# Gate and up products of the experts: stationary weights, 96 streamed slots, one-piece weight split

## The chip, the cores and the metric

One core of a Trainium2 chip runs the whole program. The metric is device time in microseconds of one execution; the median of three runs is quoted. The engines are called PE (matrix products, PEld for its weight loads), DVE (vector), ACT (scalar), POOL and SP (which issues the loads).

## The reference

Two layers over 256 latent and 256 context tokens of width 1024. Each layer has three attention branches merged by gates, then a channel mixer: a dense SwiGLU in layer 0, and in layer 1, for the latents alone, eight experts of which each token uses two:

```python
gate, up = jnp.split(h @ w_gu, 2, axis=-1)
return (jax.nn.silu(gate) * up) @ w_dn
```

Per expert w_gu is 1024 x 5632 and w_dn 2816 x 1024, in fp32. The router takes the top two of eight logits per token and weights the two outputs by a softmax over them. There are 512 assignments of a token to an expert. The result is the latents' stream after a last RMS norm.

## The kernel before, in words

Every matrix is held as two fp16 parts, high and low, and a product is three fp16 products: high by high, high by low, low by high. Weights come from memory as fp32 tiles of 128 x 2048 (1 MiB). `load_raw` (L300) issues the load on SP into the next of a ring of buffers, 12 in the expert stage. `split_w` (L308) makes the parts into one of three pairs of weight buffers (`WB`, L283): ACT writes the high part (L266), DVE the low part (L263), in two pieces of 1024 columns each. ACT, DVE and PE work on different tiles at once. The framework's planner sets each engine's order from the program; only in a few places (`issue_after`) is it written by hand.

The experts come last (L1106 to L1324). `route` (L1114) sorts tokens into slots. Then, one expert after the other:

- `gather` (L1176) builds a 0/1 matrix P of tokens by 128 slots, and with it the expert's tokens `xg`, two parts of [d, slots] (products at L1201, copies on ACT at L1203), the transposed matrix PT and the slots' weights `wsl`. The next expert's gather is called during this one's down products.
- `expert` (L1207) has 11 blocks of two weight tiles. A tile holds, for four chunks of the contraction, 256 gate and 256 up columns. The tokens are stationary (128 x 128) and 512 weight columns stream past them: 12 products a tile (L1227 to L1229), with the result [slots, 256 gate | 256 up] in one bank of PSUM. ACT takes SiLU of the gate half into `ht` (L1231), DVE multiplies by the up half (L1232, by the helper at L257). `turn` (L1213) puts the block's product on [hidden, slots] by two fp32 transposes on PE (L1216), and ACT and DVE split that into `hdh` and `hdl`. A block is turned only after the next one's products (`last`).
- Then 11 tiles of the down projection: `hdh`, `hdl` stationary, 512 columns streaming, 132 products (L1254 to L1256), and the scaled outputs `yh`, `yl` (L1258).
- `combine` (L1262) brings the outputs of up to three experts back to their tokens; its eight jobs are put between a later expert's blocks. The last expert's own follow each half of its result.

A second pass (L1327 to L1357) runs in a device loop over the experts, if some expert has more than 128 tokens.

```python
for k in range(4):
    kk = 4 * half + k
    c = slice(512 * k, 512 * k + 512)
    T.matmul(ps, xg[0][:, kk], w[0][:, c], start=(kk == 0), stop=False)
    T.matmul(ps, xg[0][:, kk], w[1][:, c], start=False, stop=False)
    T.matmul(ps, xg[1][:, kk], w[0][:, c], start=False, stop=(kk == KD - 1))
```

Of the kernel before, what the change touches and what calls it, by code (L numbers as in the profile page):

```python
# [15 lines left out]
D = 1024  # L16
# [5 lines left out]
NE = 8  # L22
VW = 416
# [9 lines left out]
# ---------------------------------------------------------------- layout of the inputs (host, no arithmetic)  # L33
# [116 lines left out]
def const_mats():  # L150
    """ident | rotation | one, heads | strictly lower | expert triangle | slots"""
# [58 lines left out]
def moe_tiles(w_gu, w_dn, w_router):  # L210
    """Per expert: 22 tiles of gate and up columns side by side, 11 tiles of the down projection, one half of its
    outputs after the other."""
    g = w_gu.reshape(NE, 2, 4, 128, 2, 11, 256)
    g = g.transpose(0, 5, 1, 3, 2, 4, 6).reshape(NE, 22, 128, 2048)
# [29 lines left out]
# ---------------------------------------------------------------- the kernel  # L244


def trunk(tc, A, out):
# [41 lines left out]
    def take(kind, slots):  # L289
        """The next of several groups of buffers, in proportion to their sizes."""  # L290
        order = [g for g in slots for _ in range(g[2])]
        g = order[turn[kind] % len(order)]
        turn[kind] += 1
        return g
# [13 lines left out]
    def split_w(raw, w, parts=None):  # L308
# [4 lines left out]
        for a in range(0, w, 1024):  # L313
            b = min(w, a + 1024)
# [13 lines left out]
    # ---- constants and small inputs  # L328
# [25 lines left out]
    # silu of the conditioning: as columns, and along every lane for the row sums  # L354
# [18 lines left out]
    def ada_tile(pool, cb, t):  # L373
        """Two column chunks of layer 1's modulation, for the latents' and (where used) the context's vector."""
# [10 lines left out]
    def ada_group(i, g):  # L385
        """The eight chunks of group g (sh1 sc1 g1 sh2 sc2 g2) are in: bias, then the form that the use needs."""
# [30 lines left out]
    def ada0_cols(row, ch):  # L417
        """The column groups' sum, put on the lanes, and the bias: chunks ch .. ch+3."""
# [7 lines left out]
    def first_mod(half):  # L426
        """Layer 0's first shift and scale, half of the chunks."""
# [128 lines left out]
    def residual(ps, d, c, gate, o=0):  # L556
        """xT chunk d, tokens c: plus the gated product."""
# [5 lines left out]
    def start(pool, nrm):  # L563
        """Layer 0's first norm and products, as its shift and scale come in."""
# [20 lines left out]
    def mixer(pool, i, ada_q, nrm, nxt, first=None):  # L585
        """One layer's three token mixers: adds the gated merge of their outputs to xT, and feeds the next norm."""
# [34 lines left out]
        # ---- first products, following the norm  # L621
# [39 lines left out]
        def bcast(rstd, tiles, s, two):  # L661
            """1/rms values of one norm, along the lanes of its chunk: [128, tokens] in PSUM."""
# [12 lines left out]
        def turned(dst, r, c):  # L675
            """The rotary turn of the latents."""
# [42 lines left out]
        # ---- values, and the rotary key of the latent-attention branch, token by token  # L719
# [32 lines left out]
        def gate0(d):  # L752
            """A chunk of the first branch's gate, kept where the merge goes."""
# [6 lines left out]
        class Latent:  # L760
            """The latent queries: projected, normed."""
# [22 lines left out]
        class Grouped:  # L784
            """Two chunks of the grouped-query branch: projected, normed by head, turned."""
# [24 lines left out]
        # ---- latent-attention branch: normed low ranks, then up  # L810
# [45 lines left out]
        # ---- attention: pairs of heads, context queries over the context, latent queries over everything  # L856
# [83 lines left out]
        # ---- a branch's output, gated (tanh of half the argument), added to the merge  # L940
# [165 lines left out]
    # ---- experts: 128 slots each; a second block of slots for the experts that are given more tokens  # L1106
# [69 lines left out]
    def gather(pool, pos_e, w_e, slots):  # L1176
        """One block of 128 slots of one expert: the scale of its outputs, its tokens in fp16 parts [d, slots], the slot
        matrix [slots, tokens]."""
        P = pool.tile([128, 2, 128], F16, tag="P", bufs=2, name=nm("P"))
        for t in range(2):  # L1180
            V.tensor_scalar(P[:, t], slots, pos_e(t), None, op0=OP.is_equal)
        PT = pool.tile([128, NLAT], F16, tag="PT", bufs=6, name=nm("PT"))
        pt = pb([128, D], F16)
        for t in range(2):
            T.transpose(pt[:, 128 * t:128 * t + 128], P[:, t], ident16)
        S.copy(PT, pt[:, :NLAT])
        pw = pb([128, 2])
        for t in range(2):
            T.matmul(pw, P[:, t], w_e(t), start=(t == 0), stop=(t == 1))
        wsl = pool.tile([128, 2], FT, tag="wsl", bufs=4, name=nm("wsl"))  # L1190
        V.tensor_copy(wsl, pw)
        V.tensor_scalar(wsl[:, 0:1], wsl[:, 0:1], wsl[:, 1:2], 1.0 / (WS * PSC), op0=OP.add, op1=OP.mult)
        xg = []
        for j in range(2):
            g = pool.tile([128, KD, 128], F16, tag="xg", bufs=4, name=nm("xg"))
            for h in range(2):
                ps = (pb if h else pa)([128, 4, 128])
# [5 lines left out]
                S.copy(g[:, 4 * h:4 * h + 4], ps)  # L1203
            xg.append(g)
        return wsl, xg, PT

    def expert(pool, wsl, xg, tile_of, jobs, meanwhile, halves=(lambda *y: None,) * 2):  # L1207
        """The block through the expert: its scaled output [slots, d] in fp16 parts. jobs: work to put between the
        first products; meanwhile: before the second ones; halves: after either half of the result."""
        hdh = pool.tile([128, NF, 128], F16, tag="hd", bufs=2, name=nm("hdh"))  # L1210
        hdl = pool.tile([128, NF, 128], F16, tag="hd", bufs=2, name=nm("hdl"))

        def turn(b, t_):  # L1213
            pt = pb([128, 2, 128])
            for j in range(2):
                T.transpose(pt[:, j], t_[:, 128 * j:128 * j + 128], ident)  # L1216
            split(hdh[:, 2 * b:2 * b + 2], hdl[:, 2 * b:2 * b + 2], pt, US * AS)

        last = None
        for b in range(11):  # L1220
            ps = pa()
            for half in range(2):
                w = tile_of(2 * b + half)
                for k in range(4):
                    kk = 4 * half + k
                    c = slice(512 * k, 512 * k + 512)
                    T.matmul(ps, xg[0][:, kk], w[0][:, c], start=(kk == 0), stop=False)  # L1227
                    T.matmul(ps, xg[0][:, kk], w[1][:, c], start=False, stop=False)  # L1228
                    T.matmul(ps, xg[1][:, kk], w[0][:, c], start=False, stop=(kk == KD - 1))  # L1229
            t_ = pool.tile([128, 256], FT, tag="ht", bufs=3, name=nm("ht"))  # L1230
            S.activation(t_, ps[:, :256], AF.Silu, scale=US)  # L1231
            mul(t_, t_, ps[:, 256:])  # L1232
            if last:
                turn(*last)
            last = b, t_
# [143 lines left out]
```

## Time and profile before

| | us |
|---|---|
| median of 3 runs | 1854.41 |
| lowest, highest | 1850.96, 1860.81 |
| span of the profiled execution | 1850.3 |
| its own run time | not listed |
| PE busy | 1745.7 |
| DVE busy | 1412.7 |
| ACT busy | 1080.2 |

The span runs from the first to the last instruction of the profiled execution. Products are pipelined, so a product's own length (379 ns at 512 columns) is longer than the distance between two starts, and busy time on PE says only that something is in flight. L12 is line 12 of the kernel. In the names of groups, numbers of buffers are left out: `wh` and `wl` are the high and low parts of a weight tile, `raw` its fp32 form.

### The profile page before, as it was taken

Reading aid. Unit: us, or ns where it says so; the run is one execution under the profiler, and the core shown is the slowest. Engines: PE = TensorE matmul, PEld = TensorE weight load, DVE = VectorE, ACT = ScalarE, POOL = GpSimd, SP = SyncE. Lnnn points to the kernel's source line nnn. Section 1 sums busy time; section 2 is a strip of 40 time slices with the busy share of each in tenths; the row PEclk is TensorE's granted clock in tenths of the full one; section 3 lists DMA queues with packets and bytes.
Section 4 is the critical chain, followed back from the end, with each engine's and each line's share of the span. In section 5 each row is a group of like instructions: output and inputs, shape, how many; then the busy total and the mean of one; then the engine's idle time right before and its main releaser. Section 6 shows DMA issues by size and latency. Waiting matters only on the chain.

```text
span 1850.3 us, 26306 instructions
## 1 busy us (share of the span) xinstructions
PE 1745.7 (94%) x9965; PEld 926.9 (50%) x9965; DVE 1412.7 (76%) x2464; ACT 1080.2 (58%) x1685; POOL 1.4 (0%) x7
## 2 busy tenths in 40 slices
PE   6998899999999999989879989999999999999996
PEld 2544444446544444476557844444445444445442
DVE  4678757356885545357787799999899999999996
ACT  3456646243333222236565578888877787877784
POOL 0000000000000000000000000000000000000000
PEclk9998999999999999999899989999999999999998
DMA  9254496552455446425377689999999999999980
GB/s 373 93 141 105 104 300 152 149 195 89 172 206 209 169 147 207 145 93 170 81 160 172 211 338 410 378 390 380 356 362 358 371 375 371 373 371 348 365 338 25
DMA packets 149942, 451.19 MB, mean 244 GB/s; under 512 B 92208, under 2 KB 95408, under 8 KB 103088
## 3 DMA queue, kind: packets, MB, share of 16 engines
q1 hardware_dynamic: 149376, 449.03, 69.1%
q8 instruction: 80, 1.31, 0.3%
q14 instruction: 54, 0.44, 0.1%
q10 hardware_dynamic: 432, 0.41, 0.1%
HBM read 427.38 MB, written 1.05 MB: 232 GB/s over the span
## 4 chain that ended last, share of the span: by engine, by line
PE 65%; DVE 14%; DMA 6%; ACT 4%; issue 3%; SPq 0%; ACTq 0%; DVEq 0%
DVE wl L263 8%; PE pg L319 6%; PE pg L320 6%; PE pg L321 6%; PE pa L1228 6%; PE pa L1229 6%; PE pa L1227 6%; PE pa L320 5%; PE pa L321 5%; PE pa L319 5%; ACT wh L266 3%; PE pg L1255 2%; DMA pt<-pn 2%; PE pg L1256 2%; PE pg L1254 2%
## 5 line engine op out<-in xcount | busy, mean ns | idle before, releaser
L263 DVE SCALAR_TENSOR_TENSOR wl<-raw,wh 128x1024 f16<-128x1024 f32 x740 | 836.3, 1174 | 69.3 <-ACT wh L266 65.6
L266 ACT ACTIVATE wh<-raw 128x1024 f16<-128x1024 f32 x740 | 710.3, 1012 | 231.5 <-PE pa L320 91.2
L1228 PE MATMUL pa<-wl,xg 128*128 128x512 f16 x704 | 266.7, 379 | 3.0 <-DVE wl L263 1.5
L1227 PE MATMUL pa<-wh,xg 128*128 128x512 f16 x704 | 267.0, 379 | 0.0
L1229 PE MATMUL pa<-wh,xg 128*128 128x512 f16 x704 | 266.8, 379 | 0.0
L319 PEld LDWEIGHTS <-wh 128*128 128x128 f16 x1530 | 152.8, 100 | 129.5 <-issue 20.3
L321 PEld LDWEIGHTS <-wl 128*128 128x128 f16 x1530 | 152.1, 99 | 117.8 <-issue 9.6
L320 PEld LDWEIGHTS <-wh 128*128 128x128 f16 x1530 | 152.0, 99 | 116.8 <-issue 10.6
L319 PE MATMUL pa<-hh,wh 128*128 128x512 f16 (+1 forms) x480 | 166.9, 354 | 8.9 <-ACT hh L537 8.9
L319 PE MATMUL pg<-hh,wh 128*128 128x512 f16 (+1 forms) x512 | 172.6, 337 | 2.9 <-DVE km L263 2.3
L320 PE MATMUL pg<-hl,wh 128*128 128x512 f16 (+1 forms) x512 | 172.2, 336 | 0.0
L321 PE MATMUL pg<-hh,wl 128*128 128x512 f16 (+1 forms) x512 | 171.5, 335 | 0.0
L320 PE MATMUL pa<-hl,wh 128*128 128x512 f16 (+1 forms) x480 | 168.9, 353 | 2.1 <-DVE hl L263 2.1
L321 PE MATMUL pa<-hh,wl 128*128 128x512 f16 (+1 forms) x480 | 168.8, 353 | 0.0
L263 DVE SCALAR_TENSOR_TENSOR scr<-raw,cb 128x1024 f16<-128x1024 f32 x64 | 78.4, 1225 | 87.0 <-DMA raw<-in_ada 85.9
L1255 PE MATMUL pg<-wl,hdh 128*128 128x512 f16 x352 | 133.3, 379 | 2.6 <-DVE wl L263 1.9
L1256 PE MATMUL pg<-wh,hdl 128*128 128x512 f16 x352 | 133.4, 379 | 0.0
L1254 PE MATMUL pg<-wh,hdh 128*128 128x512 f16 x352 | 132.7, 379 | 0.0
L1229 PEld LDWEIGHTS <-xg 128*128 128x128 f16 x704 | 68.8, 98 | 84.8 <-issue 10.7
L1227 PEld LDWEIGHTS <-xg 128*128 128x128 f16 x704 | 68.8, 98 | 78.3
L1228 PEld LDWEIGHTS <-xg 128*128 128x128 f16 x704 | 68.8, 98 | 72.5
L266 ACT ACTIVATE pn<-P,sml 128x512 f16<-128x512 f32 (+1 forms) x96 | 60.5, 645 | 32.4 <-DMA pt<-pn 19.4
(257 smaller groups left out, 2158.7 us busy)
## 6 DMA issues: line engine op xcount, KB each, us to landing
raw<-in_wm SPq DMA_DIRECT2D x264, 1024.0 KB, 7.0
raw<-in_ws SPq DMA_DIRECT2D x52, 1024.0 KB, 4.9
raw<-in_ada SPq DMA_DIRECT2D x48, 1024.0 KB, 5.5
raw<-in_ws SPq DMA_DIRECT2D x18, 768.0 KB, 5.0
raw<-in_ws SPq DMA_DIRECT2D x16, 704.0 KB, 4.2
raw<-in_ws SPq DMA_DIRECT2D x16, 640.0 KB, 4.0
raw<-in_ws SPq DMA_DIRECT2D x4, 832.0 KB, 11.3
xT<-in_xt SPq DMA_DIRECT2D x4, 512.0 KB, 6.3
```

The lines of the kernel that those rows point to most:

```text
L263: return V.scalar_tensor_tensor(o, a, s, b, op0=op0, op1=op1, **kw)
L266: h = S.activation(hi, src, AF.Copy, scale=scale)
L319: T.matmul(ps, sh, mh, start=first, stop=False)
L320: T.matmul(ps, sh, ml, start=False, stop=False)
L321: T.matmul(ps, sl, mh, start=False, stop=last)
L1227: T.matmul(ps, xg[0][:, kk], w[0][:, c], start=(kk == 0), stop=False)
L1228: T.matmul(ps, xg[0][:, kk], w[1][:, c], start=False, stop=False)
L1229: T.matmul(ps, xg[1][:, kk], w[0][:, c], start=False, stop=(kk == KD - 1))
L1254: T.matmul(py, hdh[:, f], w[0][:, c], start=(f == 0), stop=False)
L1255: T.matmul(py, hdh[:, f], w[1][:, c], start=False, stop=False)
L1256: T.matmul(py, hdl[:, f], w[0][:, c], start=False, stop=(f == NF - 1))
```

## The change

The weights of gate and up are laid out on the host in tiles of 128 hidden units: for each of the eight chunks of the contraction 128 gate columns, then the same for up. In the kernel 128 x 128 pieces of the weights become stationary, and 96 token slots stream past them: 16 pieces a tile, three products each. The result lies on [hidden, slots] at once, so `turn` and its transposes go, and SiLU, multiply and split of a block follow one another. Slots per expert are 96 (`CAP`); `P`, `PT`, `xg`, the hidden values and the outputs narrow with them. Expert weight tiles, all but the first, are split in one piece of 2048 columns. The second pass is entered above 96 tokens and loops over two blocks of slots. Comments and docstrings are removed, too.

```diff
+CAP = 96
-    g = w_gu.reshape(NE, 2, 4, 128, 2, 11, 256)
-    g = g.transpose(0, 5, 1, 3, 2, 4, 6).reshape(NE, 22, 128, 2048)
+    g = w_gu.reshape(NE, KD, 128, 2, NF, 128)
+    g = g.transpose(0, 4, 2, 3, 1, 5).reshape(NE, NF, 128, 2048)
...
-    def split_w(raw, w, parts=None):
+    def split_w(raw, w, parts=None, step=1024):
-        for a in range(0, w, 1024):
-            b = min(w, a + 1024)
+        for a in range(0, w, step):
+            b = min(w, a + step)
...
-        P = pool.tile([128, 2, 128], F16, tag="P", bufs=2, name=nm("P"))
+        P = pool.tile([128, 2, CAP], F16, tag="P", bufs=2, name=nm("P"))
...
+        xg = pool.tile([128, KD, 2, CAP], F16, tag="xg", bufs=2, name=nm("xg"))
         for j in range(2):
-            g = pool.tile([128, KD, 128], F16, tag="xg", bufs=4, name=nm("xg"))
             for h in range(2):
-                ps = (pb if h else pa)([128, 4, 128])
+                ps = (pb if h else pa)([128, 4, CAP])
...
-                S.copy(g[:, 4 * h:4 * h + 4], ps)
-            xg.append(g)
+                S.copy(xg[:, 4 * h:4 * h + 4, j], ps)
...
-        hdh = pool.tile([128, NF, 128], F16, tag="hd", bufs=2, name=nm("hdh"))
-        hdl = pool.tile([128, NF, 128], F16, tag="hd", bufs=2, name=nm("hdl"))
-        def turn(b, t_):
-            pt = pb([128, 2, 128])
+        hdh = pool.tile([128, NF, CAP], F16, tag="hd", bufs=2, name=nm("hdh"))
+        hdl = pool.tile([128, NF, CAP], F16, tag="hd", bufs=2, name=nm("hdl"))
+        for b in range(11):
+            ps = pa([128, 2, 2, CAP])
             for j in range(2):
-                T.transpose(pt[:, j], t_[:, 128 * j:128 * j + 128], ident)
-            split(hdh[:, 2 * b:2 * b + 2], hdl[:, 2 * b:2 * b + 2], pt, US * AS)
...
+                w = tile_of(2 * b + j)
+                for a in range(2):
+                    for k in range(KD):
+                        c = slice(1024 * a + 128 * k, 1024 * a + 128 * k + 128)
+                        prod(ps[:, j, a], w[0][:, c], w[1][:, c], xg[:, k, 0], xg[:, k, 1], k == 0, k == KD - 1)
+            t_ = pool.tile([128, 2, CAP], FT, tag="ht", bufs=3, name=nm("ht"))
+            S.activation(t_, ps[:, :, 0], AF.Silu, scale=US)
+            mul(t_, t_, ps[:, :, 1])
+            split(hdh[:, 2 * b:2 * b + 2], hdl[:, 2 * b:2 * b + 2], t_, US * AS)
...
-                py = pg()
+                py = pg()[:CAP]
...
-            return load_w("wm", (33 * e + t) * 128 * 2048)
+            return split_w(load_raw("wm", (33 * e + t) * 128 * 2048), 2048, step=2048)
...
-    with tc.If(most > 128):
+    with tc.If(most > CAP):
...
+            for first_slot in range(CAP, NLAT, CAP):
+                slot2 = pool.tile([128, 128], FT, tag="slot2", name=nm("slot2"))
+                V.tensor_scalar(slot2, slot, float(first_slot), None, op0=OP.add)
+                with tc.For_i(0, NE, 1) as e:
```

## Rows read from the trace of the kernel before

**Rows 1.** The page: span, busy time, and PE's busy tenths in 40 slices.

```profile
span 1850.3 us, 26306 instructions
PE 1745.7 (94%) x9965; PEld 926.9 (50%) x9965; DVE 1412.7 (76%) x2464; ACT 1080.2 (58%) x1685; POOL 1.4 (0%) x7
...
PE   6998899999999999989879989999999999999996
```

**Rows 2.** Stretches, gate/up then down: length, busy by engine, clock, DMA share, GB/s.

```profile
1176.20:1235.40 59.20, 59.20 (x286) 28.38 (x285) 58.14 (x65) 49.87 (x65) 0.00 (x0) 1.00 1.00 392
1266.60:1325.70 59.10, 59.10 (x285) 28.29 (x284) 56.76 (x63) 47.70 (x62) 0.00 (x0) 1.00 0.98 388
...
sum 494.90, PE 491.85 PEld 239.15 DVE 467.09 ACT 403.01 POOL 0.00; mean PE 61.48 PEld 29.89 DVE 58.39 ACT 50.38 POOL 0.00
...
sum 250.80, PE 247.32 PEld 118.55 DVE 227.46 ACT 195.75 POOL 0.00; mean PE 30.91 PEld 14.82 DVE 28.43 ACT 24.47 POOL 0.00
```

**Rows 3.** Timeline of PE across a block's end: start, length, line, tiles, shapes.

```profile
1298.53 0.38 PE L1216 MATMUL pb<-cmat,ht 128*128 128x128 f32 x2
1298.75 0.38 PE L1227 MATMUL pa<-wh,xg 128*128 128x512 f16 x1
...
1300.26 0.38 PE L1228 MATMUL pa<-wl,xg 128*128 128x512 f16 x1
```

**Rows 4.** Timeline of DVE, then of ACT, in the same block.

```profile
1294.96 4.63 DVE L263 SCALAR_TENSOR_TENSOR wl<-raw,wh 128x1024 f16<-128x1024 f32 x4
1299.51 0.41 DVE L257 TENSOR_TENSOR ht<-ht,pa 128x256 f32<-128x256 f32 x1
...
1300.36 2.36 DVE L263 SCALAR_TENSOR_TENSOR wl<-raw,wh 128x1024 f16<-128x1024 f32 x2
...
1296.14 2.00 ACT L266 ACTIVATE wh<-raw 128x1024 f16<-128x1024 f32 x2 [0.26 <-PE pa L1229]
1298.73 0.38 ACT L1231 ACTIVATE ht<-pa 128x256 f32<-128x256 f32 x1 [0.58 <-PE pa L1229]
```

**Rows 5.** DMA issues of the expert weights: count, size, us to landing.

```profile
raw<-in_wm SPq DMA_DIRECT2D x264, 1024.0 KB, 7.0
```

**Rows 6.** A stretch early in the kernel, columns as in rows 2.

```profile
12.00:32.00 20.00, 14.41 (x80) 7.39 (x80) 11.63 (x30) 6.97 (x11) 0.42 (x1) 0.87 1.02 429
```

**Rows 7.** Timeline of PE in layer 1: 256, 128 and 8 streamed columns.

```profile
999.95 0.27 PE L319 MATMUL pg<-hh,wh 128*128 128x256 f16 x1
...
1000.50 0.27 PE L321 MATMUL pg<-hh,wl 128*128 128x256 f16 x1
...
1058.64 0.22 PE L319 MATMUL pg<-mh,wh 128*128 128x128 f16 x1
...
1059.25 0.22 PE L321 MATMUL pg<-mh,wl 128*128 128x128 f16 x1
...
1070.44 0.17 PE L319 MATMUL pb<-wrh,hh 128*128 128x8 f16 x1 [0.30 <-DVE hu L263]
...
1070.94 0.17 PE L320 MATMUL pb<-wrl,hh 128*128 128x8 f16 x1
```

**Rows 8.** The stretch of the densest products, columns as in rows 2.

```profile
1053.09:1065.09 12.00, 11.45 (x199) 11.22 (x196) 6.41 (x26) 2.68 (x9) 0.00 (x0) 1.00 0.20 81
```

**Rows 9.** Weight splits by width: count, busy us and mean ns, idle before.

```profile
L263 DVE SCALAR_TENSOR_TENSOR wl<-raw,wh 128x1024 f16<-128x1024 f32 x686 | 807.0, 1221 | 69.3 <-ACT wh L266 65.6
...
L263 DVE SCALAR_TENSOR_TENSOR wl<-raw,wh 128x256 f16<-128x256 f32 x16 | 6.7, 418 | 0.0
...
L266 ACT ACTIVATE wh<-raw 128x1024 f16<-128x1024 f32 x686 | 686.1, 1050 | 231.5 <-PE pa L320 91.2 <-issue 57.1 <-PE pg L320 51.3
...
L266 ACT ACTIVATE wh<-raw 128x256 f16<-128x256 f32 x16 | 6.4, 400 | 0.0
```

**Rows 10.** Waits in the expert stage (1084 to 1826): us, times, longest.

```profile
DVE wl L263 <- ACT wh L266: 35.2, 86, 1.5
...
PEld L1229 <- issue: 10.7, 28, 0.6
```

More of the change, by code (lines that the diff above doesn't have):

```diff
@@ L1176, in gather @@
     def gather(pool, pos_e, w_e, slots):
-        P = pool.tile([128, 2, 128], F16, tag="P", bufs=2, name=nm("P"))
+        P = pool.tile([128, 2, CAP], F16, tag="P", bufs=2, name=nm("P"))
         for t in range(2):
-            V.tensor_scalar(P[:, t], slots, pos_e(t), None, op0=OP.is_equal)
-        PT = pool.tile([128, NLAT], F16, tag="PT", bufs=6, name=nm("PT"))
+            V.tensor_scalar(P[:, t], slots[:, :CAP], pos_e(t), None, op0=OP.is_equal)
+        PT = pool.tile([CAP, NLAT], F16, tag="PT", bufs=6, name=nm("PT"))
         pt = pb([128, D], F16)
         for t in range(2):
-            T.transpose(pt[:, 128 * t:128 * t + 128], P[:, t], ident16)
-        S.copy(PT, pt[:, :NLAT])
-        pw = pb([128, 2])
+            T.transpose(pt[:CAP, 128 * t:128 * t + 128], P[:, t], ident16)
+        S.copy(PT, pt[:CAP, :NLAT])
+        pw = pb([128, 2])[:CAP]
         for t in range(2):
             T.matmul(pw, P[:, t], w_e(t), start=(t == 0), stop=(t == 1))
-        wsl = pool.tile([128, 2], FT, tag="wsl", bufs=4, name=nm("wsl"))
+        wsl = pool.tile([CAP, 2], FT, tag="wsl", bufs=4, name=nm("wsl"))
         V.tensor_copy(wsl, pw)
         V.tensor_scalar(wsl[:, 0:1], wsl[:, 0:1], wsl[:, 1:2], 1.0 / (WS * PSC), op0=OP.add, op1=OP.mult)
-        xg = []
+        xg = pool.tile([128, KD, 2, CAP], F16, tag="xg", bufs=2, name=nm("xg"))
         for j in range(2):
-            g = pool.tile([128, KD, 128], F16, tag="xg", bufs=4, name=nm("xg"))
             for h in range(2):
-                ps = (pb if h else pa)([128, 4, 128])
+                ps = (pb if h else pa)([128, 4, CAP])
                 for k in range(4):
@@ L1202, in gather @@
                                  start=(t == 0), stop=(t == 1))
-                S.copy(g[:, 4 * h:4 * h + 4], ps)
-            xg.append(g)
+                S.copy(xg[:, 4 * h:4 * h + 4, j], ps)
         return wsl, xg, PT
     def expert(pool, wsl, xg, tile_of, jobs, meanwhile, halves=(lambda *y: None,) * 2):
-        hdh = pool.tile([128, NF, 128], F16, tag="hd", bufs=2, name=nm("hdh"))
-        hdl = pool.tile([128, NF, 128], F16, tag="hd", bufs=2, name=nm("hdl"))
-        def turn(b, t_):
-            pt = pb([128, 2, 128])
+        hdh = pool.tile([128, NF, CAP], F16, tag="hd", bufs=2, name=nm("hdh"))
+        hdl = pool.tile([128, NF, CAP], F16, tag="hd", bufs=2, name=nm("hdl"))
+        for b in range(11):
+            ps = pa([128, 2, 2, CAP])
             for j in range(2):
-                T.transpose(pt[:, j], t_[:, 128 * j:128 * j + 128], ident)
-            split(hdh[:, 2 * b:2 * b + 2], hdl[:, 2 * b:2 * b + 2], pt, US * AS)
[L1219 to L1235, printed above, removed]
+                w = tile_of(2 * b + j)
[7 more added lines that the diff above has]
+            split(hdh[:, 2 * b:2 * b + 2], hdl[:, 2 * b:2 * b + 2], t_, US * AS)
             if jobs:
@@ L1239, in expert @@
             jobs.pop(0)()
-        yh = pool.tile([128, D], F16, tag="yh", bufs=4, name=nm("yh"))
-        yl = pool.tile([128, D], F16, tag="yl", bufs=4, name=nm("yl"))
+        yh = pool.tile([CAP, D], F16, tag="yh", bufs=4, name=nm("yh"))
+        yl = pool.tile([CAP, D], F16, tag="yl", bufs=4, name=nm("yl"))
         res = None
@@ L1246, in expert @@
                 w = tile_of(22 + j // 4)
-            if j == 0:
-                turn(*last)
             if j == 12:
@@ L1326, in trunk @@
     most = nc.values_load(cnti[0:1, 0:1], min_val=0, max_val=NLAT)
-    with tc.If(most > 128):
+    with tc.If(most > CAP):
         with tc.tile_pool(name="mo2", bufs=1) as pool, tc.tile_pool(name="dr", bufs=1,
                                                                     space=bass.MemoryType.DRAM) as dp:
-            slot2 = pool.tile([128, 128], FT, name="slot2")
-            V.tensor_scalar(slot2, slot, 128.0, None, op0=OP.add)
             dpos = dp.tile([NE, 128, 2], FT, name="dpos")
@@ L1337, in trunk, with tile_of @@
             wm = A["wm"].rearrange("(e t p n) -> e t p n", e=NE, t=33, p=128)
-            with tc.For_i(0, NE, 1) as e:
-                pe = pool.tile([128, 2], FT, name="pe")
-                we = pool.tile([128, 2, 2], F16, name="we")
-                nc.sync.dma_start(pe, dpos[ds(e, 1)].rearrange("o p t -> (o p) t"))
-                nc.sync.dma_start(we.rearrange("p a b -> p (a b)"), dsel[ds(e, 1)].rearrange("o p t -> (o p) t"))
-                def tile_of(t):
-                    raw = new_raw()
-                    nc.sync.dma_start(raw, wm[ds(e, 1), t].rearrange("o p n -> (o p) n"))
-                    return split_w(raw, 2048)
-                wsl, xg, PT = gather(pool, lambda t: pe[:, t:t + 1], lambda t: we[:, t, :], slot2)
-                yh, yl, _ = expert(pool, wsl, xg, tile_of, [], lambda: None)
-                for job in combine([(yh, yl, PT)]):
-                    job()
+            for first_slot in range(CAP, NLAT, CAP):
+                slot2 = pool.tile([128, 128], FT, tag="slot2", name=nm("slot2"))
+                V.tensor_scalar(slot2, slot, float(first_slot), None, op0=OP.add)
+                with tc.For_i(0, NE, 1) as e:
+                    pe = pool.tile([128, 2], FT, tag="pe", name=nm("pe"))
+                    we = pool.tile([128, 2, 2], F16, tag="we", name=nm("we"))
+                    nc.sync.dma_start(pe, dpos[ds(e, 1)].rearrange("o p t -> (o p) t"))
+                    nc.sync.dma_start(we.rearrange("p a b -> p (a b)"), dsel[ds(e, 1)].rearrange("o p t -> (o p) t"))
+                    def tile_of(t):
+                        raw = new_raw()
+                        nc.sync.dma_start(raw, wm[ds(e, 1), t].rearrange("o p n -> (o p) n"))
+                        return split_w(raw, 2048)
+                    wsl, xg, PT = gather(pool, lambda t: pe[:, t:t + 1], lambda t: we[:, t, :], slot2)
+                    yh, yl, _ = expert(pool, wsl, xg, tile_of, [], lambda: None)
+                    for job in combine([(yh, yl, PT)]):
+                        job()
             nrm = Norm(1, 0, [(2, 4)])
```

## The prediction, on record before the result

> **What bounds the kernel now.** I read the page first, for where time goes. Its first two parts [rows 1] show PE busy 94% of the span, and at 9 tenths through the 15 slices before the last: the expert stage, where all that the change touches lies. The page's other engines are at 76% and 58%. An average over the span says nothing about it, so I cut that stage into stretches, by the start of each expert's first gate product (L1227) and first down product (L1254). The eight gate/up stretches add up to 494.9 us, the eight down stretches to 250.8 us [rows 2]; 745.7 us in all, 93.2 us an expert. In gate/up PE is busy 491.9 of 494.9 us and DVE 467.1; in down PE 247.3 of 250.8 and DVE 227.5. So PE ends every stretch, with DVE close behind in the first kind (94%).
>
> One block (two tiles) shows both at once. On PE a 512-column product starts every 0.216 us (1298.75 to 1300.26 is seven steps) and the pair of transposes takes 0.22 us [rows 3]. A block is 24 products and one pair: 24 x 0.216 + 0.22 = 5.40 us. On DVE [rows 4] four low halves start at 1294.96 and the multiply starts at 1299.51, so each half costs 4.55 / 4 = 1.14 us of DVE's time, less than its 1.22 us because it overlaps the next; then 0.85 us for the multiply and the low part of the hidden values: 5.40 us from one block to the next. DVE has almost nothing spare: in the plain gate/up stretch from 1176.2 it is busy 58.1 of 59.2 us [rows 2].
>
> DMA is third. The 264 loads of 1 MiB [rows 5] run at 388 to 392 GB/s in the plain gate/up stretches [rows 2], but early in the kernel, with many loads queued, 429 GB/s [rows 6]; there a tile costs 1.049 MB / 429 = 2.45 us, 33 tiles 80.7 us, against 93.2 us now.
>
> **The change, part by part.** *Gate and up products.* Now a tile costs 12 products of 512 columns, 12 x 0.216 = 2.59 us; then it costs 48 products of 96 columns, each with a weight load of its own. No row has 96 columns. With a weight load before each product, 256 columns pace at 0.110 us (999.95 to 1000.50, five steps), 128 at 0.056 (1058.64 to 1059.25, eleven steps) and 8 at 0.027 (1070.44 to 1070.94, nineteen steps) [rows 7]. The line through the first two gives 0.056 - 32 x 0.42 ns = 0.043 us at 96; the bounds are 0.027 below and 0.056 above. I take 0.043, since 128 columns is the near row: 48 x 0.043 = 2.06 us a tile, 22 tiles 45.4 us an expert instead of 57.0.
>
> These products start twice as often as any long stretch here shows. The densest long one, 12 us of out-projection, started 199 in 12.0 us, 0.060 us each [rows 8], gaps and a few foreign instructions included, so a pace of 0.043 held through 45 us is my extension. The Trainium skill, "TensorE: Matmul & The Clock Gate", section "Wait — 56ns, not 53.3ns?", says that an engine whose sequencer decodes matmuls itself spends about 62 ns on each and that this binds once the array's work is shorter. No run here shows it: 56 ns [rows 7] lies below it, but over runs that a filled queue could carry. By that figure 48 products would be an estimated 2.98 us a tile, and the stage some 45 us longer than now; by the rows it is 2.06 us.
>
> *Transposes gone.* 88 pairs of 0.22 us leave PE (19 us in sum, inside the 5.40 above). Their two PSUM copies become two operations on the SBUF product. The hidden values' operations narrow from 256 to 192 columns. By the widths [rows 9], DVE's slope is (1221 - 418) / 768 = 1.05 ns a column, so the multiply and the low part save 0.067 us each, 0.134 a block.
>
> *One split instead of two.* DVE's 1024-column low part takes 1221 ns, ACT's high part 1050 [rows 9]; extended along their slopes, 2048 columns cost 2292 and 1917 ns. Back to back two DVE halves take 2.28 us and one whole piece 2.29 - 0.08 of overlap = 2.21: 0.07 us a tile less, bounds 0 and 0.15 (the whole fixed part, 418 - 256 x 1.05 = 149 ns; a loss is excluded, since the narrow pieces are the dearer ones per column [rows 9]). 263 tiles change, 18 us of DVE. ACT saves about as much, and is covered (403 of 494.9 us [rows 2]). The price is delay: DVE may start only after 1.9 us of ACT instead of 1.0. With three weight buffers a buffer's round is 1.92 + 2.21 + 2.06 + about 0.4 of handoffs = 6.6 us, or 2.2 a tile, under DVE's 2.5; in down, with 2.59 for PE, 7.1 us, 2.4 a tile, under PE's 2.59. So it is hidden; were DVE faster, this would be the bound.
>
> *96 slots.* Gather's 32 products an expert go from 0.056 to 0.043, 0.4 us. Down keeps its 512 streamed columns and its 0.216 us; the loss of the last transposes gives 0.2 us more. The overflow block is not entered: the reference's own router, evaluated on its drawn inputs, gives the fullest expert 82 of 512 assignments, below 96 as below 128, and there were just 8 x 33 loads [rows 5]. The queues keep their order: SP still issues 264 loads, each waiting for the last reader of its buffer, which is one DVE instruction instead of the second of two. PE's instructions grow by 8 x 22 x 36 pairs; their code loads are hidden as long as PE waits for DVE anyway. PE's "issue" waits now are 10.7 us at L1229 [rows 10]; with cover gone I count up to 18 us, from the same mean of 0.38 us at some 50 more code loads.
>
> *The new wait.* Before, the transposes of a block were held back until the next block, so ACT's and DVE's work on hidden values was one block late and never urgent. Now SiLU, multiply, high part, low part follow in one block, and alternate between ACT and DVE. Behind a waiting high part on ACT stands the next tile's high half, and DVE waits for that. The nearest row is DVE's present wait for ACT's high halves: 35.2 us in 86 waits, 0.41 each [rows 10]. One such per block would be 88 x 0.41 = 36 us; bounds 0 and 36 (below nothing is excluded, a wait gives no time back); I take half, 18 us.
>
> **The sum.** Gate/up becomes DVE's: 467.1 - 176 x 0.07 - 88 x 0.134 = 443.0 us. Down stays PE's: 250.8 - 8 x 0.6 = 246.0 us (DVE's 227.5 less 8 us is under it). Together 689.0 us, 57 less than 745.7; with 18 us of the new wait, 39 us less. In down DVE can run up to two tiles ahead, which gate/up then uses; at most it brings the stage to DVE's own total, 467.1 + 227.5 - 18 - 12 = 664.6, another 24 us. I leave this out of the sum and keep it in the range. DMA's 8 x 80.7 = 646 us stays under all of these. The profiled execution's span is 1850.3 us [rows 1], and its own run time is not listed; the median of three runs is 1854.4, 4.1 above the span, and I keep that distance: 1850.3 - 39 + 4.1 = 1815 us.
>
> **The rivals.** *The forecast*, PE relieved and DVE the new bound: 1773 (no new wait, full lead: 81 us) to 1833 (36 us of wait, no lead), or 1851 with the uncovered code loads. For it: PE at 99.4% of gate/up now. Chance 0.70.
>
> *The gain is eaten by the chain inside the block.* If each block costs DVE about 0.65 us, as when a wait of 0.41 is joined by a shorter one at the low part, 88 x 0.65 = 57 us go and the time is 1854. For it: DVE has no slack to hide a wait any more. Against it: ACT is 81% busy and can run ahead. Chance 0.12, 0.03 of it past the loss bound.
>
> *PE cannot start products that fast (the loss).* Place: the gate/up products. It decides from 0.052 us a product, where 48 of them reach DVE's 443.0 / 176 = 2.52 us a tile, and turns to a loss at 59.4 / (22 x 48) = 0.056, the PE time of gate/up now (22 x 2.59 and 11 pairs). At 0.060 [rows 8] a tile costs 2.88 us, gate/up 63.4 instead of 59.4, less 0.6 in down: 8 x 3.4 = 27 us more, 1882 us. For it: no long stretch here is faster. Against it: that stretch held 0.056 wherever the gaps left it alone [rows 7], with equal loads between. Chance 0.11. The Trainium skill's page named above would have it so.
>
> *ACT's order locks the block.* If the new order puts a block's high part before the next tile's high half on ACT, and DVE its multiply behind a low part of 2.2 us, a block costs two low parts, then multiply, high part, high half in series: 4.4 + 0.3 + 0.35 + 1.9 = 7.0 us against 5.40, 88 x 1.6 = 141 us, about 1990 us. Against it: today ACT's high halves at 1296.14 end 0.6 us before the SiLU that stands behind them [rows 4], so it runs ahead of PE. Chance 0.05.
>
> *The change does not do what it says*: the overflow loop runs after all (16 more passes of some 93 us, over 3000 us), 0.01; or nothing moves, 1854 us, 0.01.
>
> **How the numbers follow.** Faster 0.70 is the forecast; the same is 0.09 of the eaten gain and 0.01 of no effect; slower is 0.03 + 0.11 + 0.05 + 0.01 = 0.20. Half a percent, some 9 us, is what a measurement of this kernel can tell from no change (the three runs lie 9.9 us apart). The range reaches from 1778 to 1860: the forecast's own bounds with nearly its best end, the code loads, and the eaten gain; it leaves out the two slow rivals.
>
> **What would show it.** Right: gate/up of an expert without combine near 55 to 57 us with DVE at 97% and PE below 85%; gate/up products of 96 columns starting 0.043 us apart; one low part of about 2.29 us a tile; down still 30 to 31 us with PE full; no load count but 264. Wrong: products 0.06 apart; many waits of DVE's low or hidden part for ACT; PE idle in down; DMA above 420 GB/s with ACT waiting for loads.

## The result, and the profile after

The changed kernel takes 1801.5 us (median of four runs, 1798.4 to 1812.0); the kernel before, beside it, 1853.2 (1851.0 to 1860.8). The ratio is 0.972 [0.969, 0.976]: faster by 52 us, where 39 were forecast. The profiled execution's span fell from 1850.3 to 1796.4 us. These are the lines of the page that answer to [rows 1], with the one on code loads:

```profile
span 1796.4 us, 38098 instructions
PE 1650.2 (92%) x16125; PEld 1086.6 (60%) x16125; DVE 1378.0 (77%) x2201; ACT 1039.5 (58%) x1422; POOL 1.4 (0%) x7
PE   6998899999999999999778988999999999999995
...
q8 instruction: 128, 2.10, 0.5%
```

By share of the span PE is still the busiest engine, and its digits read 9 in the 14 slices before the last. The limit is seen only in the stretches, cut as in [rows 2]. First two plain gate/up stretches (the second and third expert), then the sum of all eight of gate/up, then that of all eight of down:

```profile
1173.80:1228.00 54.20, 49.78 (x1103) 47.39 (x1102) 53.75 (x46) 47.20 (x48) 0.00 (x0) 1.00 1.01 415
1258.80:1312.40 53.60, 48.78 (x1073) 46.05 (x1072) 53.39 (x44) 46.06 (x45) 0.00 (x0) 1.00 1.01 419
...
sum 444.70, PE 403.60 PEld 379.96 DVE 436.89 ACT 378.13 POOL 0.00; mean PE 50.45 PEld 47.49 DVE 54.61 ACT 47.27 POOL 0.00
...
sum 247.80, PE 239.90 PEld 137.05 DVE 222.35 ACT 180.41 POOL 0.00; mean PE 29.99 PEld 17.13 DVE 27.79 ACT 22.55 POOL 0.00
```

Gate/up fell from 494.9 to 444.7 us, down from 250.8 to 247.8: 53.2 us together, nearly all of the 53.9 in the span. In the third expert DVE is now busy 53.39 of 53.6 us and PE 48.78. DMA share is 1.01 at 415 to 419 GB/s, so two suspects stand full beside each other, DVE and the loads. The experiments have to part them.

The timeline shows a block. PE first, over 0.8 us of gate/up products:

```profile
1290.82 0.21 PE L321 MATMUL pa<-xg,wh 128*128 128x96 f16 x1
1290.86 0.21 PE L322 MATMUL pa<-xg,wl 128*128 128x96 f16 x1
...
1291.58 0.21 PE L321 MATMUL pa<-xg,wh 128*128 128x96 f16 x1
```

From 1290.82 to 1291.58 are 18 steps, 0.042 us each. DVE in the same block:

```profile
1290.58 0.34 DVE L258 TENSOR_TENSOR ht<-ht,pa 128x192 f32<-128x192 f32 x1
1290.85 2.28 DVE L264 SCALAR_TENSOR_TENSOR wl<-raw,wh 128x2048 f16<-128x2048 f32 x1
1293.05 0.35 DVE L264 SCALAR_TENSOR_TENSOR hdl<-ht,hdh 128x192 f16<-128x192 f32 x1
1293.32 2.28 DVE L264 SCALAR_TENSOR_TENSOR wl<-raw,wh 128x2048 f16<-128x2048 f32 x1
1295.52 0.34 DVE L258 TENSOR_TENSOR ht<-ht,pa 128x192 f32<-128x192 f32 x1
```

A block is 1295.52 - 1290.58 = 4.94 us against 5.40 in [rows 4]: two low parts at 2.20 from start to start (1290.85 to 1293.05), and 0.27 each for the multiply and the hidden low part. None of these rows has an idle time before it. DVE makes a whole weight tile's low part between the multiply and the hidden low part, so the in-block chain, which needs ACT between the two, costs DVE nothing. It shows on ACT:

```profile
1290.96 0.36 ACT L267 ACTIVATE hdh<-ht 128x192 f16<-128x192 f32 x1 [0.76 <-DVE ht L258]
1291.23 1.90 ACT L267 ACTIVATE wh<-raw 128x2048 f16<-128x2048 f32 x1
1293.03 0.31 ACT L1220 ACTIVATE ht<-pa 128x192 f32<-128x192 f32 x1
1293.24 1.90 ACT L267 ACTIVATE wh<-raw 128x2048 f16<-128x2048 f32 x1
```

ACT stands 0.76 us a block before the hidden high part. The weight's high part behind it ends at 1293.13, and DVE's low part of that weight starts at 1293.32: 0.19 us to spare. The waits of the expert stage (1080 to 1780; total us, times, longest):

```profile
PEld L322 <- DVE wl L264: 57.5, 136, 1.4
ACT hdh L267 <- DVE ht L258: 57.3, 75, 1.7
...
ACT yh L267 <- PE pg L1241: 26.6, 15, 5.6
DVE wl L264 <- ACT wh L267: 19.1, 38, 1.8
PEld L1241 <- issue: 12.4, 20, 1.3
PE pg L1240 <- DVE wl L264: 7.4, 14, 1.0
...
ACT wh L267 <- DMA raw<-in_wm: 4.3, 6, 1.0
```

PE now waits for DVE's low parts (57.5 us). DVE's wait for ACT's high parts, of which the forecast wanted more, fell from 35.2 us [rows 10] to 19.1.

### The profile page after: what moved, and what is told of

Same layout as the page of the kernel before. It is cut to its first block, busy times and chain, and to the rows that moved or that the text cites. A ratio compares the mean times of both kernels' runs of the same rounds, so it can differ in the third digit from the quotient of the medians.

```text
span 1796.4 us, 38098 instructions
## 1 busy us (share of the span) xinstructions
PE 1650.2 (92%) x16125; PEld 1086.6 (60%) x16125; DVE 1378.0 (77%) x2201; ACT 1039.5 (58%) x1422; POOL 1.4 (0%) x7
## 4 chain that ended last, share of the span: by engine, by line
PE 45%; DVE 18%; issue 12%; DMA 12%; ACT 5%; ACTq 0%; SPq 0%; DVEq 0%
DVE wl L264 10%; DMA raw<-in_wm 7%; PE pg L320 6%; PE pg L321 6%; PE pg L322 6%; PE pa L321 6%; PE pa L322 6%; PE pa L320 5%; DMA pt<-pn 3%; ACT wh L267 3%; PE pg L1240 2%; PE pg L1241 2%; PE pg L1239 2%; PE pb L935 1%; DVE ht L258 1%
## 5 line engine op out<-in xcount | busy, mean ns | idle before, releaser
L264 DVE SCALAR_TENSOR_TENSOR wl<-raw,wh 128x2048 f16<-128x2048 f32 (+1 forms) x477 | 820.9, 1735 | 54.6 <-ACT wh L267 50.6
L267 ACT ACTIVATE wh<-raw 128x2048 f16<-128x2048 f32 (+1 forms) x477 | 686.9, 1462 | 260.1 <-PE pa L321 93.1
L322 PEld LDWEIGHTS <-wl 128*128 128x128 f16 x4346 | 428.1, 99 | 176.6 <-DVE wl L264 58.0
L320 PEld LDWEIGHTS <-wh 128*128 128x128 f16 x4346 | 429.4, 99 | 133.3 <-issue 19.0
L321 PEld LDWEIGHTS <-wh 128*128 128x128 f16 x4346 | 428.6, 99 | 117.1 <-issue 9.6
L322 PE MATMUL pa<-xg,wl 128*128 128x96 f16 x2816 | 375.7, 207 | 37.0 <-DVE wl L264 36.5
L320 PE MATMUL pa<-xg,wh 128*128 128x96 f16 x2816 | 374.7, 206 | 3.7 <-ACT wh L267 3.7
L321 PE MATMUL pa<-xg,wh 128*128 128x96 f16 x2816 | 374.6, 206 | 0.0
L1240 PE MATMUL pg<-wl,hdh 128*96 128x512 f16 x352 | 133.4, 379 | 7.9 <-DVE wl L264 7.4
L1241 PE MATMUL pg<-wh,hdl 128*96 128x512 f16 x352 | 133.3, 379 | 0.0
L1239 PE MATMUL pg<-wh,hdh 128*96 128x512 f16 x352 | 132.2, 379 | 0.0
L321 PE MATMUL pg<-dl,wh 128*128 128x512 f16 (+1 forms) x198 | 70.4, 355 | 0.0
```

The lines of the kernel that those rows point to most:

```text
L264: return V.scalar_tensor_tensor(o, a, s, b, op0=op0, op1=op1, **kw)
L267: h = S.activation(hi, src, AF.Copy, scale=scale)
L320: T.matmul(ps, sh, mh, start=first, stop=False)
L321: T.matmul(ps, sh, ml, start=False, stop=False)
L322: T.matmul(ps, sl, mh, start=False, stop=last)
L1239: T.matmul(py, hdh[:, f], w[0][:, c], start=(f == 0), stop=False)
```

## The experiments

"Stage" below is the time in the profiled execution from the start of expert 0's first gate product to the end of the last down product: 745.6 us before, 692.7 after. The three questions are what each part of the change brings, what bounds gate/up now, and whether a better version is near. Each ratio is to the kernel before on the same chip; its median was 1853.2 us beside the changed kernel and 1856.2 to 1859.0 beside the experiments, so that ratios and stages compare better than times.

**1. The parts of the change.** The changed kernel with the weight tiles split in two pieces again:

```
-  return split_w(load_raw("wm", ...), 2048, step=2048)
+  return split_w(load_raw("wm", ...), 2048)
```

> The changed kernel with the split of expert weights back in two pieces of 1024 columns. Theory (DVE is the new bound of gate/up): two low pieces cost DVE 2 x 1.136 = 2.27 us instead of 2.20, so 176 gate/up tiles lose 12 us; down, bound by PE, loses nothing: about 1813 us. Rival (the longer whole pieces delay PE, so the one-piece split costs a wait): the time stays at 1801 or falls below.

Measured: 1816.2 us, ratio 0.980 [0.976, 0.984]; stage 705.2, 12.5 longer, about the 12 expected. Its parts differ more. In expert 0 PE makes the first down product with 3.7 us of gate/up products still to come. With these counted to gate/up, it takes 462.9 us in all, 18 longer, and down takes 242.3, 5.5 shorter. DVE's timeline in the third expert:

```profile
1295.00 3.49 DVE L264 SCALAR_TENSOR_TENSOR wl<-raw,wh 128x1024 f16<-128x1024 f32 x3
1298.41 0.34 DVE L258 TENSOR_TENSOR ht<-ht,pa 128x192 f32<-128x192 f32 x1
```

Three pieces take 1298.41 - 1295.00 = 3.41 us, so a tile of two 2.27 against 2.20: the 0.07 of the forecast, 1.5 us an expert. But the third expert's gate/up takes 57.2 us, 3.6 longer. The run changes more than the piece: ACT's order from expert 2 on has SiLU behind the high part of one tile that follows, not of two, and PE waits 1.8 us for low parts in down, not 7.4. The price of the pieces is shown in DVE's pace; how much of the 12.5 us comes with the order is not.

The kernel before with the single piece alone:

```
-  return load_w("wm", (33 * e + t) * 128 * 2048)
+  return split_w(load_raw("wm", (33 * e + t) * 128 * 2048), 2048, step=2048)
```

> The kernel before with nothing but the split in one piece of 2048 columns. Theory: a block stays at PE's 5.40 us, so nothing is gained, 1848 to 1858 us; DVE's busy time in the stage falls by about 18 us and turns into idle time. Rival (the cheaper split is what pays): 1838 us or less.

Measured: 1855.5, ratio 0.9995 [0.998, 1.001]. The split whose undoing costs the changed kernel 12.5 us of its stage brings no gain that can be told from noise while PE is the bound.

The changed kernel with 128 slots, and with 88:

```
-CAP = 96
+CAP = 128
```

> The changed kernel with 128 slots instead of 96. Theory: 48 products at 0.056 us are 2.69 us a tile, over DVE's 2.5, so PE is the bound of gate/up again: 22 x 2.69 = 59 us an expert plus the combine, the stage about 733 us and the time about 1841 us. Rival (the streamed columns don't matter; the gain is the dropped transposes or the split): about 1803 us.

Measured: 1841.5, ratio 0.992 [0.990, 0.995]; stage 732.2, gate/up 487.9. These are the products with DVE's low parts, a third of all, in this run and in the changed kernel (count, busy, mean ns, idle before):

```profile
L322 PE MATMUL pa<-xg,wl 128*128 128x128 f16 x2816 | 473.5, 219 | 1.2 <-DVE wl L264 1.2
...
L322 PE MATMUL pa<-xg,wl 128*128 128x96 f16 x2816 | 375.7, 207 | 37.0 <-DVE wl L264 36.5
```

With 128 slots PE waits 1.2 us for low parts, with 96 it waits 37.0: at 128 PE is the bound again, at 59.0 us a plain expert. So the narrower stream carries some 40 us of the gain (732.2 - 692.7 of the stage), and what is left, some 13, comes with the rest of the change.

```
-CAP = 96
+CAP = 88
```

> The changed kernel with 88 slots instead of 96. Theory: DVE bounds gate/up, so only its two narrower operations per block count, 88 x 2 x 16 x 1.05 ns = 3 us: about 1798 us. Rival (PE still bounds gate/up): 8448 products lose 8 columns, 3.3 ns each, 28 us: about 1773 us.

Measured: 1799.9, ratio 0.970 [0.966, 0.973]; stage 689.8, 2.9 less. Were PE the bound, 8 columns less would be 8 x 0.42 ns x 8448 products = 28 us. From 128 to 96 columns the time falls with PE; from 96 to 88 it doesn't: the limit changes hands between the two.

**2. DVE or the loads?** First DVE's work was halved, the low part made for the first 1024 columns only and used twice:

```
+  S.activation(hi, raw, AF.Copy, scale=WS)
+  stt(lo[:, :1024], raw[:, :1024], WS, hi[:, :1024], OP.mult, OP.subtract)
...
-  prod(..., w[0][:, c], w[1][:, c], ...)
+  prod(..., w[0][:, c], w[1][:, cl], ...)
```

> The changed kernel with the low part of an expert weight tile made for its first 1024 columns only; the products of the second half take those again (so the second half's low part is left out of the computation). PE, ACT and the loads keep their work, DVE loses 1.07 us a tile. Theory (DVE is the bound of gate/up, and the loads stand just behind it): the stage falls from 692 us to the loads' 8 x 80.8 = 647 us and stays there: about 1757 us. Rival A (the loads are the bound already): 1790 us or more. Rival B (PE still is): about 1800 us.

Measured: 1837.2, ratio 0.988 [0.985, 0.990], 36 us slower than the changed kernel with less work: a miss by 80 us. Its stage is 728.0. Experts 0 and 1 take 55.3 and 52.4 us of gate/up, later ones 62 to 64. The two differ in ACT's order: in most blocks of experts 0 and 1 the SiLU of a block stands behind the high parts of three tiles that follow; from the end of expert 1 on behind one. The changed kernel has three, then two. The order comes from the planner. I tried to undo it by writing SiLU, multiply and split of a block after the next block's products in the program:

```
+  if last:
+      hidden(*last)
+  last = b, ps
-  S.activation(t_, ps[:, :, 0], AF.Silu, scale=US)
-  mul(t_, t_, ps[:, :, 1])
-  split(hdh[:, 2 * b:2 * b + 2], hdl[:, 2 * b:2 * b + 2], t_, US * AS)
```

> The kernel of the half low part, with SiLU, multiply and split of a block written into the program after the next block's products (the second half's low part is left out of the computation as there). Theory (there the engines were not the bound, but ACT's order: SiLU stood ahead of the next tile's high part, so high part, low part, products and SiLU followed in series, 5.6 us a block): ACT then runs ahead, the stage falls to 650 to 665 us, where the loads end it: about 1765 us. Rival (DVE is not what holds gate/up, so its saved work can't show): 1800 us or more.

Measured: 1837.5, ratio 0.990 [0.987, 0.993], another miss. The planner put SiLU in the same place as in the run without the move. But the run shows both orders with the same work. First ACT's timeline early in expert 1, then in expert 2, then expert 2's stretch and two of its waits:

```profile
1178.71 0.31 ACT L1220 ACTIVATE ht<-pa 128x192 f32<-128x192 f32 x1
1178.92 1.90 ACT L322 ACTIVATE wh<-raw 128x2048 f16<-128x2048 f32 x1
...
1182.77 0.31 ACT L1220 ACTIVATE ht<-pa 128x192 f32<-128x192 f32 x1
...
1294.85 0.33 ACT L1220 ACTIVATE ht<-pa 128x192 f32<-128x192 f32 x1 [1.43 <-PE pa L329]
1295.07 1.90 ACT L322 ACTIVATE wh<-raw 128x2048 f16<-128x2048 f32 x1
...
1300.45 0.33 ACT L1220 ACTIVATE ht<-pa 128x192 f32<-128x192 f32 x1 [1.43 <-PE pa L329]
```

```profile
1255.00:1317.70 62.70, 49.51 (x1074) 46.30 (x1073) 33.59 (x45) 47.06 (x45) 0.00 (x0) 1.00 1.00 396
...
ACT ht L1220 <- PE pa L329: 14.6, 10, 1.7
PEld L329 <- DVE wl L264: 12.5, 11, 1.1
```

With SiLU late ACT doesn't wait here, and a block takes 1182.77 - 1178.71 = 4.06 us (for as long as stocked loads last: two tiles in 4.06 us are over 500 GB/s). With SiLU early ACT stands 1.43 us in each block until PE has ended the block; only then it makes the high part from which the next low part and PE's next tile follow. That loop through ACT, DVE and PE takes 1300.45 - 1294.85 = 5.60 us a block, and expert 2 needs 62.7 us with no engine busy above 50. The loads are not what it waits for: ACT's and DVE's waits for them came to 7.3 us in the whole stage of the run before the move. The same late place in the changed kernel itself:

> The changed kernel with nothing but that later place of SiLU, multiply and split in the program. Theory (DVE has low parts to make between these steps, so the chain inside a block costs it nothing): 1798 to 1806 us. Rival (the chain costs DVE a wait in each block): 1790 us or less.

Measured: 1802.9, ratio 0.972 [0.968, 0.975]. The number is as expected, but the run doesn't test the theory: the engines' instructions stand in the same order as in the changed kernel, and the stretches are its own (444.9 and 247.9 us).

Then the loads were halved, with DVE's work left whole; half of each tile is loaded and read twice:

```
+  nc.sync.dma_start(raw[:, :1024], bass.AP(..., ap=[[2048, 128], [1, 1024]]))
...
+  src = raw[:, None, :1024].to_broadcast([128, 2, 1024])
+  issued[0] = split(two(hi), two(lo), src, WS)
```

> The changed kernel with only the first 1024 columns of each expert weight tile loaded, and used for both halves of the tile (so half of the experts' weights is left out of the computation). ACT, DVE and PE keep their work; the bytes halve. Theory (DVE bounds gate/up, PE bounds down, the loads only follow): 1793 to 1801 us. Rival (the loads are the bound at 415 GB/s): 1770 us or less.

Measured: 1795.3, ratio 0.965 [0.963, 0.967]; stage 687.1. Its second and third expert in gate/up:

```profile
1177.90:1231.30 53.40, 48.35 (x1057) 45.42 (x1056) 53.19 (x41) 45.80 (x42) 0.00 (x0) 1.00 0.63 214
1262.30:1315.70 53.40, 48.35 (x1057) 45.45 (x1056) 53.19 (x41) 45.82 (x42) 0.00 (x0) 1.00 0.64 214
```

With half the bytes (214 GB/s, share 0.64) a plain expert takes 53.4 us instead of 53.6, and DVE is busy 53.19 of it. Full DMA engines cost the changed kernel some 0.2 us there; most of the 5.6 us that the stage gains lies in expert 0 (57.7 instead of 61.2 us of gate/up) and in down (246.0 instead of 247.8). The pair to this run halves both, with the late place as well:

```
+  two = raw[:, None, :1024].to_broadcast([128, 2, 1024])
+  issued[0] = S.activation(hi.rearrange("p (a b) -> p a b", a=2), two, AF.Copy, scale=WS)
+  stt(lo[:, :1024], raw[:, :1024], WS, hi[:, :1024], OP.mult, OP.subtract)
```

> As the half low part with the later place, and only the first 1024 columns of each expert weight tile loaded and used twice (both halves of the weights' work are left out of the computation as before). Theory (behind DVE stand the loads, behind them PE with 45 + 31 = 76 us an expert): the stage falls to 610 to 630 us: about 1730 us. Rival (the loads were not the second bound): as with all loads, about 1765 us.

Measured: 1726.7, ratio 0.931 [0.928, 0.934]; stage 619.3. Here the planner left SiLU behind three tiles almost throughout, as in the run before. Its third expert, and the sum of its gate/up:

```profile
1239.40:1284.20 44.80, 44.80 (x1057) 44.80 (x1056) 32.27 (x42) 44.65 (x42) 0.00 (x0) 1.00 0.76 251
...
sum 376.70, PE 374.22 PEld 372.19 DVE 269.14 ACT 363.41 POOL 0.00; mean PE 46.78 PEld 46.52 DVE 33.64 ACT 45.43 POOL 0.00
```

Between these two runs the loads are alike and DVE's low part is halved: 53.4 becomes 44.8 us an expert. DVE is the bound of gate/up in the changed kernel, shown by taking its work away. With DVE relieved PE is busy for every one of the 44.8 us: 1056 products, 44.8 / 1056 = 0.0424 us each, with no longer gap between two starts. ACT, busy 44.65 us, stands level with it.

**3. Versions that might be faster.** With DVE the bound, its hidden low part was moved to POOL:

```
-  mul(t_, t_, ps[:, :, 1])
-  split(hdh[...], hdl[...], t_, US * AS)
+  stt(t_, t_, US * AS, ps[:, :, 1])
+  S.activation(hdh[...], t_, AF.Copy)
+  G.tensor_tensor(hdl[...], t_, hdh[...], op=OP.subtract)
```

> The changed kernel with the low part of the hidden values made by POOL instead of DVE (the scale moves into DVE's multiply). Theory: DVE loses 88 x 0.27 = 24 us in gate/up, which it bounds; the loads leave room for about 20 of these: about 1782 us. Rival A (gate/up is not bound by DVE): 1801 us. Rival B (POOL's work holds up DVE or comes too late for the down products): 1801 us or more.

Measured: 1815.2, ratio 0.976 [0.973, 0.978]: a miss, 14 us slower than the changed kernel instead of 20 faster. POOL's line group in the expert stage, then a stretch of DVE's and of POOL's timeline, and last a place where POOL started with no low part running:

```profile
L1223 POOL TENSOR_TENSOR hdl<-ht,hdh 128x192 f16<-128x192 f32 x88 | 185.7, 2110 | 1240.3 <-ACT hdh L1222 1240.3
```

```profile
1289.33 2.28 DVE L264 SCALAR_TENSOR_TENSOR wl<-raw,wh 128x2048 f16<-128x2048 f32 x1
1291.64 2.52 DVE L264 SCALAR_TENSOR_TENSOR wl<-raw,wh 128x2048 f16<-128x2048 f32 x1
1294.09 0.34 DVE L264 SCALAR_TENSOR_TENSOR ht<-ht,pa 128x192 f32<-128x192 f32 x1
1294.36 4.84 DVE L264 SCALAR_TENSOR_TENSOR wl<-raw,wh 128x2048 f16<-128x2048 f32 x2
...
1289.89 2.13 POOL L1223 TENSOR_TENSOR hdl<-ht,hdh 128x192 f16<-128x192 f32 x1 [2.89 <-ACT hdh L1222]
...
1714.74 0.55 POOL L1223 TENSOR_TENSOR hdl<-ht,hdh 128x192 f16<-128x192 f32 x1 [33.78 <-ACT hdh L1222]
1714.91 2.53 DVE L264 SCALAR_TENSOR_TENSOR wl<-raw,wh 128x2048 f16<-128x2048 f32 x1
```

POOL's subtraction has a mean of 2.11 us, but most of that is not its own work. At 1714.74 it takes 0.55 us, against DVE's 0.35. At 1289.89 it starts inside a running low part and ends at 1292.02, 0.41 after that low part (1289.33 + 2.28 = 1291.61). 72 of the 88 take some 2.1 us in this way. The low part that runs first keeps its 2.28 us; the next one starts at 1291.64, without the 0.08 of overlap, and takes 2.52. So the two engines hold each other up, and the one that starts first keeps its length. The pair of low parts takes 4.83 us (1294.16 - 1289.33), where 2 x 2.28 - 0.08 = 4.48 would do. DVE saves the 0.27 of the hidden low part and loses 0.35 on the pair: a block from 1289.33 to 1294.36 is 5.03 us, not 4.94. The stage is 698.0, 5.3 longer.

How large the loss is in all is less sure than the 14 us look. The kernel before took 1859.0 us beside this run, 5.7 more than beside the changed kernel; by the ratios (0.976 and 0.972) the loss is some 7 us, and their intervals overlap. The stage explains most of that. The profiled execution of this run also reached the stage at 1095.5 us, where the others did so at 1083.1 to 1093.5; work ahead of the stage varies by that much in unchanged code.

A fourth weight buffer pair in place of a load buffer, so that DVE can run further ahead in down:

```
-  raw_slots.extend([(px, "raw3", 1), (pool, "raw2", 5)])
+  raw_slots.extend([(px, "raw3", 1), (pool, "raw2", 4)])
+  wb_slots.append((pool, "v", 1))
```

> The changed kernel with a fourth pair of weight buffers in the expert stage and 11 instead of 12 load buffers. Theory: in down, which PE bounds, DVE waits for a free weight buffer; one more lets it run one tile of 2.2 us further ahead per expert, which gate/up then saves: 8 x 2.2 = 18 us at most, with the loads close behind: about 1788 us. Rival (DVE's lead doesn't carry over, the two stages add): 1801 us.

Measured: 1798.5, ratio 0.968 [0.965, 0.971]; stage 686.8. Only experts 0 and 1 gain (57.0 and 52.0 us of gate/up instead of 61.2 and 54.2, while down is 0.8 longer in all); from expert 2 on it is 53.7, as without it. One wait grew instead, on ACT:

```profile
ACT yh L267 <- PE pg L1241: 58.1, 15, 5.6
```

It was 26.6 us. ACT waits there for the down output, and in its order the next high parts stand behind; that this is what keeps DVE from using the fourth buffer is argued from the order, not shown by a run.

Last, both cheap edits together, the fourth pair and 88 slots:

> The changed kernel with four weight buffers and 88 slots, the two sizes that came out a little lower by themselves. Theory: DVE's narrower operations give 3 us, the first two experts' head start 4 to 6 us: about 1795 us, 0.4% under the changed kernel. Rival (both were noise): 1801 us.

Measured, median of six executions: 1793.3 (1789.4 to 1799.8), ratio 0.967 [0.964, 0.969]; stage 682.4. It is the lowest of the kernels that leave nothing out, below either edit alone (1798.5 and 1799.9), but its interval touches the changed kernel's [0.969, 0.976] and the two were not measured on one chip together: a gain over the changed kernel of half a percent is likely and not established.

## Why the prediction was right, and where it was off

The forecast's mechanism held: PE relieved, DVE the next bound. The time, 1801.5, lies 13 us under the 1815 forecast and inside the range.

- **Gate and up products.** Forecast 0.043 us each, by a line through 256 and 128 columns. Measured 0.042, and 0.0424 through 1056 in a row, where PE never stands still in an expert. The rival with 0.060 is refuted. At a granted clock of 1.00 (2.4 GHz) the Trainium skill, "TensorE: Matmul & The Clock Gate", section "Wait — 56ns, not 53.3ns?", gives 96 / 2.4 GHz + 2.5 ns, an estimated 42.5 ns, and the trace agrees; the 62 ns of the same section, that of a sequencer decoding for itself, doesn't hold here.
- **One split.** Forecast 0.07 us a tile, nothing while PE is the bound. With two pieces DVE's pace is 2.27 a tile against 2.20, as forecast, and the single piece alone brought nothing. The 12.5 us of the run with two pieces fit too, but ACT's order changed with it, so the sum is not a clean price.
- **DVE's total in gate/up.** Forecast 443.0. The stretches came to 444.7, but as 436.9 of work and 7.8 of idle time, of which 6.2 lies in expert 0. That the two totals agree is in part luck: the work fell by 30.2 us and not by 24.1, and the idle time made up for it. Most of the excess is in the hidden values' two operations. DVE's line before, between the multiply at 1299.51 and the next low part at 1300.36 of [rows 4]:

```profile
1299.84 0.42 DVE L263 SCALAR_TENSOR_TENSOR hdl<-pb,hdh 128x256 f16<-128x256 f32 x1
```

It ended at 1300.26, and DVE stood 0.10 us. So the 0.85 of the forecast were 0.75 of work, and the hidden low part overlapped nothing behind it. After the change the two take 0.54 from start to start: 0.21 less, where 0.134 was reckoned, and 88 x 0.08 is some 7 us, near the 6.1 of excess.

- **The new wait: the term that was mis-sized.** It was priced at 18 us, half of "one such per block". In its place DVE stood idle 1.6 us in the seven experts after the first, and its wait for ACT's high parts in the whole stage fell by 16. The chain is real: ACT stands 0.76 us a block in it (57.3 us in 75 waits). But DVE has a low part of 2.2 us to do meanwhile, and the next high part comes 0.19 us before it is wanted. The forecast said that behind ACT's wait stands DVE's next operand; it didn't count what DVE holds in hand at that moment. By its terms the stage's stretches were to be 443.0 + 18 + 246.0 = 707.0 us, and they are 692.5: the difference of 14.5 is the 18, less 1.7 in gate/up and 1.8 in down.
- **Down.** Forecast 246.0, measured 247.8. PE waits 7.4 us there for low parts, and only 1.8 with two pieces, where down is 242.3: the single piece's later start, which the forecast called hidden, costs something here, though ACT's other order in that run may have a share.
- **Code loads.** Some 50 more were reckoned: packets of the instruction queue rose from 80 to 128. Uncovered they might have cost 18 us. But the weight loads' waits for "issue" in the stage came to some 13 us, 12.4 of them in down (L1241); before they had come to some 19, 10.7 of them in gate/up. That these waits are the code loads is the forecast's reading; no run shows it.
- **DMA.** Forecast under everything, and it is, by little: 33 tiles of 1.049 MB at 419 GB/s are an estimated 82.6 us, and the third expert took 85.3 (53.6 of gate/up, 31.7 of down). ACT waited 4.3 us for loads in the whole stage.
- **ACT's order.** The rival with 0.05 didn't happen in the changed kernel. In milder form it happened in two of the experiments (5.60 us a block), where I hadn't reckoned with it. Why the planner moves SiLU forward was not examined: with halved loads SiLU stands behind three tiles throughout, but so it does with 128 slots and whole loads; with two pieces it stands behind one.

In sum a plain expert's gate/up had PE's 59.2 us as its limit; now it has DVE's 53.6; behind that stand ACT's order, the loads (3% under DVE over a whole expert), and PE's 44.8 us with ACT's 44.65 beside it.

## What to carry to other kernels

A wait between two engines costs nothing as long as the bounding engine holds a piece of other work in that gap; read the timeline for what it does between the two ends of a new chain, and price only what sticks out. When one bound is lifted by a tenth, list the next two or three before building on it: here DVE came to lie 9% below the old PE bound and the loads 3% below DVE, so that cutting DVE's work further could bring little by itself, and halving both brought 75 us. And where a planner sets the order, an edit that takes work away can change the order of what is left, as when half the low parts made the kernel 36 us slower: compare the instruction order before reading a time as a price.

## What was not expected of the hardware

Two sizes of weight load have different durations; the line groups of the changed kernel in the expert stage:

```profile
L321 PEld LDWEIGHTS <-wh 128*128 128x128 f16 x2816 | 276.3, 98 | 0.8
...
L1240 PEld LDWEIGHTS <-hdh 128*96 128x96 f16 x352 | 43.3, 123 | 30.0
```

96 columns of weights take 123 ns, 128 take 98. In down the 512-column products, 0.216 us each [rows 3], hide it. The Trainium skill, "TensorE: Matmul & The Clock Gate", section "Weight-path perf modes — Fast Weight Load (FWL) and DoubleRow", says that the fast load is used when there are 128 weights; the rows agree in direction, and no run here shows more.

A low part on DVE and a subtraction on POOL hold each other up, though they share no buffer. POOL's took 0.55 us when it started first and some 2.1 when it started inside a low part; a low part took 2.28 us when it started first and 2.52 when POOL was still at work.
